# Order of the combinations of h, of the seven products and of the background steps in a hybrid decoder trunk

## The chip, the cores and the metric

The kernel runs on one core of a Trainium2 chip. The metric is the device time of one execution in microseconds (us), the median of several runs. TensorE is called PE in the views, VectorE DVE, ScalarE ACT, GpSimd POOL and SyncE SP; PEld is TensorE's weight load.

## The reference

One layer of a decoder trunk, for 1024 tokens and 16 meta tokens in front of them (1040 rows), model width 1024, all in float32:

```python
h = rmsnorm(concat(meta, x))
glu_a, glu_b, z_conv, q, f, i, g_rec, m_conv, m_rec = split(h @ w_in)      # nine parts of 1024 columns
y_conv = (silu(LN(causal_dwconv31(glu_a * sigmoid(glu_b)))) * silu(z_conv)) @ w_conv_out
y_rec  = (GroupRMSNorm(HGRN2(q, f, i)) * silu(g_rec)) @ w_rec_out          # 8 heads of 128
out    = rmsnorm(x + (sigmoid(m_conv) * y_conv + sigmoid(m_rec) * y_rec) @ w_out)
```

HGRN2 is a gated linear recurrence: per head a forget gate F = lb + (1 - lb) * sigmoid(f), K = 1 - F, q = silu(q_raw), and a state that is worked out in chunks of 64 rows.

## The kernel before, in words

**Products in float32.** Each operand is split into a high part, rounded to fp32r, and the rest. A product is three fp32r matmuls: high by high, low by high, high by low (L320, L323, L324 in `project`; L876, L879, L880 in the units). h is held transposed as eight pairs `hh[k]`, `hl[k]` of 128 x 1056; the columns are the rows of the sequence, in two halves of 528 (LH) up to 1056 (LX).

**Weights.** `load_w` loads a tile of 512 KB into `wraw` (SP, L149, two buffers); ACT makes `whi` (L139) and `-whi` in `wlo` (L140), and a DMA of POOL adds `wraw` to `wlo` in flight (L141). A wraw buffer is free again when that DMA has landed. `whi` and `wlo` have three buffers each.

**Plain jobs.** A list of jobs is worked off in order: for each of eight heads `f_job` (forget gate: sigmoid on ACT, L575, two operations on DVE, L576 and L578) and `q_job` (QD, ACT L596, DVE L597), between them `v_job`s, and at last two tiles of the glu part, `gb_job` and `ga_job` (product with the sigmoid, DVE L640). Each runs `project` over two or four blocks of columns with banks of PSUM from a ring of four. The loads of the next job are issued before a job is executed. After each triple of matmuls `tick` adds its length (3 n / 2400 us for n columns) to counters, and steps three queues of background work: `bg`, the heads of HGRN2 (one step each HG_GAP), whose small matmuls (L342 and others) stand in TensorE's order between the triples and wait for DVE's QD, QX, QY (L377 to L421); `cbg`, the taps of the convolution (DVE, L648, 1024 columns each, 31 to a tile); and `sbg`, `weight_sums` (one DMA each SUM_GAP). A head ends with a normalisation on DVE (L527, tile `on`), transposes on TensorE (L537), a copy on ACT (L538) and a store on POOL (L539, `oT_d`). All steps left of the heads are taken by `drained`, ahead of the last `ga_job`.

**Seven products for eight.** The gate parts (g_rec, m_rec; z_conv, m_conv) and the last six tiles of the glu part are worked out in units, two tiles by two halves of the rows at once, by a Strassen-like scheme with seven products (`strassen`). It needs combinations of the weights and of h. `weight_sums` makes those of the weights in DRAM: loads by SP (L718) and accumulating DMAs by POOL (L720), into `sum_rec`, `sum_glu`, `sum_z`. `h_sums(k)` for k = 0 to 3 makes those of h: it loads two tiles `ha`, `hb` (SP, L733, L734), combines them on DVE (L738 to L741), splits four results on ACT and DVE (L135, L136, tile `tsum`) and stores them to `t_d` 4 to 7 (POOL, L745). `h_load` loads t6, t5 and t4 back (POOL, L753); `h_last` puts t7 over the second half of `hh[k]`, `hl[k]`, k = 0 to 3 (POOL, L760, L761), which no job after the plain ones reads otherwise.

A unit's pieces of weights come by `take`: load (SP, L829), then split on ACT and DVE (L135, L136), or on ACT and a DMA of POOL (L139, L140, L141), seven pieces ahead. The products follow each other in a list (`product(0)` to `product(6)`); after some of them an output leaves through `put`: in the gate units outputs 0 and 1 take a silu (L965) and 2 and 3 a sigmoid (L975), in the glu units 0 and 1 a sigmoid (L941). Silu and sigmoid stand in different tables of ACT; an ACT_TABLE_LOAD stands ahead of each change.

After the units follow the three output projections and the last norm. The order on each engine is fixed when the kernel is built, from the order in which the program lists its work.

Of the kernel before, what the change touches and what calls it, by code (L numbers as in the profile page):

```python
# [13 lines left out]
ALU = mybir.AluOpType  # L14
# [8 lines left out]
LH = 528  # L23
# [10 lines left out]
HG_GAP = 1.85  # L34
CONV_RATE = 0.64
SUM_GAP = 2.4
# [8 lines left out]
def hybrid_kernel(ctx: ExitStack, tc: tile.TileContext, xT, xtok, wv, wp, wro, wco, wout, prm, fg, msk, out):  # L45
# [586 lines left out]
    def ga_job(j):  # L632
        def run(w):
            a = glu.pop(j)
            for blk in project(w, hh, hl, FB):
                yield
                if blk is None:
                    continue
                o, n, ps = blk
                TT(out=a[:, o:o + n], in0=a[:, o:o + n], in1=ps[:, 0:n], op=ALU.mult)  # L640
            conv_start(j, a)
        return run
# [106 lines left out]
    def h_load():  # L749
        for i in (6, 5, 4):  # L750
            for k in range(4):
                t = slot(f"t{i}_{k}", dt=F32R)
                nc.gpsimd.dma_start(out=t, in_=t_d[i][k])  # L753
                tt[i].append(t.rearrange("p (a n) -> p a n", a=2))
        yield

    def h_last():

        for k in range(4):
            nc.gpsimd.dma_start(out=hh[k][:, LH:LX], in_=t_d[7][k][:, 0:LH])  # L760
            nc.gpsimd.dma_start(out=hl[k][:, LH:LX], in_=t_d[7][k][:, LH:LX])  # L761
# [6 lines left out]
    jobs.append(([], h_sums(0)))  # L768
    jobs.append(([], h_sums(1)))
    for j in range(NC):  # L770
        jobs.append(([wp[4, j]], f_job(j)))
        if j == 0:
            jobs.append(([], h_sums(2)))
            jobs.append(([], h_sums(3)))
        jobs.append(([wp[3, j]], q_job(j)))
# [82 lines left out]
    def strassen(m0, cols, put):  # L858
# [43 lines left out]
        Y = banks()  # L902
        yield from product(3, Y, t7)
        w = tmp()
        for c in C:
            TT(out=w[c], in0=v[c], in1=Y[c], op=ALU.add)
        Z = banks()
        yield from product(4, Z, tcomb(5))
        for c in C:
            TT(out=w[c], in0=w[c], in1=Z[c], op=ALU.add)  # L910
            put(3, c, w[c])
        yield from product(5, Y, tcomb(4), False)
        u = tmp()
        for c in C:
            TT(out=u[c], in0=v[c], in1=Y[c], op=ALU.add)
            put(2, c, u[c])
        yield from product(6, Z, b22, False)
        for c in C:
            TT(out=v[c], in0=v[c], in1=Z[c], op=ALU.add)
            put(1, c, v[c])  # L920
# [60 lines left out]
    def add_pair(kind, j, fn):  # L981
# [3 lines left out]
        pieces.extend([a[0, 0], s[1], a[0, 1], s[2], s[0], a[1, 1], s[3]])  # L985
# [187 lines left out]
    h_last()  # L1173
# [149 lines left out]
```

## Time and profile before

| | us |
|---|---|
| three runs | 1268.52, 1276.27, 1275.67 |
| median | 1275.67 |
| the profiled execution | 1267.29 |
| its span in the trace | 1265.5 |
| TensorE busy in the span | 1171.3 |
| DVE, ACT, POOL busy | 874.9, 564.5, 289.9 |

All times below are of that one profiled execution and count from the start of its span. The plain jobs run to about 507 us, the units from there to about 980, the output projections to the end. "Idle before, releaser" is the time that an engine stood still ahead of an instruction, and what it waited for last. PEclk is the clock granted to TensorE, as a share of full speed.

### The profile page before, as it was taken

The numbers are of one execution on the slowest core, as the hardware profiler recorded it, in microseconds if no ns is written. First come the engines' busy times: TensorE is split into PE (matmuls) and PEld (weight loads), VectorE is DVE, ScalarE is ACT, GpSimd is POOL, SyncE is SP. The second block draws the span as 40 slices with busy tenths as digits, with TensorE's granted clock in tenths as the row PEclk, the third lists the DMA queues.
The fourth block names the chain that finished last, engine by engine and source line by source line (L and its number), as shares of the span: only waits on it lengthen the run. The fifth ranks groups of instructions, "written<-read, shape, count | busy, mean of one in ns | idle before, by whom it ended". The sixth has DMA issues, their size and how long they took to land.

```text
span 1265.5 us, 21745 instructions
## 1 busy us (share of the span) xinstructions
PE 1171.3 (93%) x8376; PEld 1011.6 (80%) x8376; DVE 874.9 (69%) x1501; ACT 564.5 (45%) x1043; POOL 289.9 (23%) x376
## 2 busy tenths in 40 slices
PE   8939999999979998769999999999999999999997
PEld 7937788988968898547888888979898778788886
DVE  7547766366355669786799999498989747645444
ACT  7544442433314431336666756666665325222211
POOL 5242120321222131422222223222233131000000
PEclk9978999999989998779999999999999989999999
DMA  6498594898596993999999989989899986445421
GB/s 222 154 285 318 157 223 137 182 240 213 110 251 151 244 193 67 349 289 245 232 244 240 252 221 243 229 200 226 213 225 314 342 233 238 162 128 170 147 88 50
DMA packets 119223, 266.54 MB, mean 211 GB/s; under 512 B 12112, under 2 KB 12496, under 8 KB 119120
## 3 DMA queue, kind: packets, MB, share of 16 engines
q0 software_dynamic: 49264, 123.16, 43.7%
q1 hardware_dynamic: 60496, 125.07, 29.6%
q10 hardware_dynamic: 9360, 16.94, 3.6%
q8 instruction: 65, 1.06, 0.3%
q14 instruction: 38, 0.31, 0.1%
HBM read 169.04 MB, written 95.81 MB: 209 GB/s over the span
## 4 chain that ended last, share of the span: by engine, by line
PE 60%; DMA 14%; DVE 13%; issue 8%; POOL 2%; ACT 2%; SPq 0%; POOLq 0%; DVEq 0%; ACTq 0%
PE mm L320 6%; PE mm L323 6%; PE mm L324 6%; PE hg L876 4%; PE hg L880 4%; PE hg L879 4%; PE mm L876 4%; PE mm L880 4%; PE mm L879 4%; DMA wlo<-wraw 2%; DMA wl<-wr 2%; PE mm L204 2%; PE mm L206 2%; PE mm L205 2%; DVE QX L386 1%
## 5 line engine op out<-in xcount | busy, mean ns | idle before, releaser
L648 DVE SCALAR_TENSOR_TENSOR c<-glu,pt,c 128x1024 f32<-128x1024 f32 (+9 forms) x240 | 306.3, 1278 | 3.5
L320 PE MATMUL mm<-hh,whi 128*128 128x264 f32 (+2 forms) x512 | 164.5, 322 | 21.6 <-ACT F L575 21.2
L141 POOL DMA_DIRECT2D wl<-wr x129 | 111.3, 903 | 312.1 <-ACT wl L140 236.8
L323 PE MATMUL mm<-hl,whi 128*128 128x264 f32 (+2 forms) x512 | 162.5, 318 | 0.3 <-DVE hl L559 0.3
L324 PE MATMUL mm<-hh,wlo 128*128 128x264 f32 (+2 forms) x512 | 161.5, 316 | 0.0
L139 ACT CAST wh<-wr 128x512 fp32r<-128x512 f32 x129 | 79.1, 619 | 111.3 <-PE hg L879 43.0
L320 PEld LDWEIGHTS mm<-hh,whi 128*128 128x128 f32 x512 | 98.1, 192 | 27.9 <-ACT F L575 21.4
L323 PEld LDWEIGHTS mm<-hl,whi 128*128 128x128 f32 x512 | 98.3, 192 | 5.9 <-DVE hl L559 0.7
L324 PEld LDWEIGHTS mm<-hh,wlo 128*128 128x128 f32 x512 | 98.2, 192 | 5.8
L876 PE MATMUL hg<-hh,wh 128*128 128x512 f32 (+1 forms) x224 | 79.7, 356 | 12.1 <-DMA hh<-t_d 12.1
L880 PE MATMUL hg<-hh,wl 128*128 128x512 f32 (+1 forms) x224 | 79.8, 356 | 4.7 <-DVE wl L136 3.8
L135 ACT CAST wh<-wr 128x512 fp32r<-128x512 f32 x63 | 38.6, 619 | 97.4 <-PE mm L323 36.2
L140 ACT ACTIVATE wl<-wh 128x512 fp32r<-128x512 f32 x129 | 79.3, 627 | 4.4 <-DMA gr<-gmr_d 2.2
L876 PE MATMUL mm<-hh,wh 128*128 128x512 f32 (+1 forms) x224 | 78.2, 349 | 1.8 <-ACT wh L135 0.8
L879 PE MATMUL hg<-hl,wh 128*128 128x512 f32 (+1 forms) x224 | 79.9, 357 | 0.0
L880 PE MATMUL mm<-hh,wl 128*128 128x512 f32 (+1 forms) x224 | 77.9, 349 | 0.4 <-DVE wl L136 0.3
L879 PE MATMUL mm<-hl,wh 128*128 128x512 f32 (+1 forms) x224 | 77.8, 347 | 0.0
L141 POOL DMA_DIRECT2D wlo<-wraw x24 | 23.0, 956 | 205.3 <-ACT wlo L140 104.4
L876 PE MATMUL hg<-t,wh 128*128 128x512 f32 (+1 forms) x168 | 59.4, 354 | 2.3 <-ACT wh L135 2.1
L879 PE MATMUL hg<-t,wh 128*128 128x512 f32 (+1 forms) x168 | 59.1, 352 | 0.0
L880 PE MATMUL mm<-t,wl 128*128 128x512 f32 (+1 forms) x168 | 58.4, 348 | 0.6 <-DMA wl<-wr 0.6
L880 PE MATMUL hg<-t,wl 128*128 128x512 f32 (+1 forms) x168 | 58.9, 350 | 0.0
(346 smaller groups left out, 3126.3 us busy)
## 6 DMA issues: line engine op xcount, KB each, us to landing
wl<-wr POOLq DMA_DIRECT2D x129, 256.0 KB, 5.1
wr<-in_wp_dram SPq DMA_DIRECT2D x66, 256.0 KB, 3.9
wlo<-wraw POOLq DMA_DIRECT2D x24, 512.0 KB, 5.6
wraw<-in_wp_dram SPq DMA_DIRECT2D x20, 512.0 KB, 6.6
t_d<-tsum POOLq DMA_DIRECT2D x16, 528.0 KB, 6.7
sum_rec<-in_wp_dram SPq DMA_DIRECT2D x16, 512.0 KB, 11.4
sum_z<-in_wp_dram SPq DMA_DIRECT2D x16, 512.0 KB, 10.3
wr<-sum_rec SPq DMA_DIRECT2D x32, 256.0 KB, 4.8
```

The source lines that it names most:

```text
L135: act.copy(out=hi, in_=src)
L139: act.copy(out=hi, in_=src)
L140: act.activation(out=lo, in_=hi.bitcast(F32), func=AF.Copy, scale=-1.0)
L141: nc.gpsimd.dma_start(out=lo, in_=src, accum_op=ALU.add)
L204: pe.matmul(ps, lhsT=a, rhs=whi, start=first, stop=False, **kw)
L320: mm = pe.matmul(ps[:, 0:n], lhsT=a, rhs=xh[k][:, o:o + n], start=(k == 0), stop=False)
L323: pe.matmul(ps[:, 0:n], lhsT=a, rhs=xl[k][:, o:o + n], start=False, stop=False)
L324: last[:] = [pe.matmul(ps[:, 0:n], lhsT=b, rhs=xh[k][:, o:o + n], start=False, stop=(k == KT - 1))]
L648: dve.scalar_tensor_tensor(out=dst, in0=a[:, p0 - d:L - d], scalar=cw[:, j, TAPS - 1 - d:TAPS - d], in1=dst, op0=ALU.mult, op1=ALU.add)
L876: mm = pe.matmul(ps[c], lhsT=a, rhs=xh, start=start and k == 0, stop=False, skip_group_check=True)
L879: pe.matmul(ps[c], lhsT=a, rhs=xl, start=False, stop=False, skip_group_check=True)
L880: pe.matmul(ps[c], lhsT=b, rhs=xh, start=False, stop=k == 3, skip_group_check=True)
```

## The change

Six edits:

- `HG_GAP` goes from 1.85 to 2.0 and `SUM_GAP` from 2.4 to 2.05.
- `h_sums(0)` and `h_sums(1)` move from ahead of `f_job(0)` to behind it, `h_sums(2)` and `h_sums(3)` from behind `f_job(0)` to behind `q_job(0)`.
- `ga_job` takes its blocks of columns from the last to the first.
- `h_last` is called from `h_load`, between t5 and t4 in the program, no longer right ahead of the units.
- The products are listed as 0, 1, 2, then t5, t7, b22, t4 (before: t7, t5, t4, b22); the outputs leave in the order 0, 3, 1, 2 (before: 0, 3, 2, 1).
- The pieces of weights are listed in the order of the products.

```diff
-HG_GAP = 1.85
+HG_GAP = 2.0
-SUM_GAP = 2.4
+SUM_GAP = 2.05
...
     def ga_job(j):
...
-            for blk in project(w, hh, hl, FB):
+            for blk in project(w, hh, hl, FB[::-1]):
...
     def h_load():
-        for i in (6, 5, 4):
+
+        for i in (6, 5, 7, 4):
             for k in range(4):
+                if i == 7:
+                    h_last(k)
+                    continue
...
-    def h_last():
-
-        for k in range(4):
-            nc.gpsimd.dma_start(out=hh[k][:, LH:LX], in_=t_d[7][k][:, 0:LH])
-            nc.gpsimd.dma_start(out=hl[k][:, LH:LX], in_=t_d[7][k][:, LH:LX])
+    def h_last(k):
+        nc.gpsimd.dma_start(out=hh[k][:, LH:LX], in_=t_d[7][k][:, 0:LH])
+        nc.gpsimd.dma_start(out=hl[k][:, LH:LX], in_=t_d[7][k][:, LH:LX])
...
-    jobs.append(([], h_sums(0)))
-    jobs.append(([], h_sums(1)))
     for j in range(NC):
         jobs.append(([wp[4, j]], f_job(j)))
         if j == 0:
+            jobs.append(([], h_sums(0)))
+            jobs.append(([], h_sums(1)))
+        jobs.append(([wp[3, j]], q_job(j)))
+        if j == 0:
             jobs.append(([], h_sums(2)))
             jobs.append(([], h_sums(3)))
-        jobs.append(([wp[3, j]], q_job(j)))
...
-        Y = banks()
-        yield from product(3, Y, t7)
+        Z = banks()
+        yield from product(3, Z, tcomb(5))
         w = tmp()
         for c in C:
-            TT(out=w[c], in0=v[c], in1=Y[c], op=ALU.add)
-        Z = banks()
-        yield from product(4, Z, tcomb(5))
+            TT(out=w[c], in0=v[c], in1=Z[c], op=ALU.add)
+        Y = banks()
+        yield from product(4, Y, t7)
         for c in C:
-            TT(out=w[c], in0=w[c], in1=Z[c], op=ALU.add)
+            TT(out=w[c], in0=w[c], in1=Y[c], op=ALU.add)
             put(3, c, w[c])
-        yield from product(5, Y, tcomb(4), False)
+        yield from product(5, Z, b22, False)
         u = tmp()
         for c in C:
-            TT(out=u[c], in0=v[c], in1=Y[c], op=ALU.add)
-            put(2, c, u[c])
-        yield from product(6, Z, b22, False)
+            TT(out=u[c], in0=v[c], in1=Z[c], op=ALU.add)
+            put(1, c, u[c])
+        yield from product(6, Y, tcomb(4), False)
         for c in C:
-            TT(out=v[c], in0=v[c], in1=Z[c], op=ALU.add)
-            put(1, c, v[c])
+            TT(out=v[c], in0=v[c], in1=Y[c], op=ALU.add)
+            put(2, c, v[c])
...
-        pieces.extend([a[0, 0], s[1], a[0, 1], s[2], s[0], a[1, 1], s[3]])
+        pieces.extend([a[0, 0], s[1], a[0, 1], s[0], s[2], s[3], a[1, 1]])
...
-    h_last()
```

**ACT, at the first forget gate.** Before, the splits of `h_sums(0)` and of `h_sums(1)` (L135) and the casts of a weight (L139, L140) stood ahead of the sigmoids of `f_job(0)` (L575):

```order
80 L135 CAST tsum<-t_821 128x528
81 L139 CAST whi<-wraw 128x1024
82 L140 ACTIVATE wlo<-whi 128x1024
83 L135 CAST tsum<-hb 128x528
84 L135 CAST tsum<-ha 128x528
85 L135 CAST tsum<-hb 128x528
86 L135 CAST tsum<-t_853 128x528
87 L575 ACT_TABLE_LOAD
88 L575 ACTIVATE F<-mm 128x264 x2
89 L575 ACTIVATE F<-mm 128x256 x2
```

Now, the sigmoids come first, then the first block of `q_job(0)` (L596) and `h_sums(0)`:

```order
77 L575 ACT_TABLE_LOAD
78 L575 ACTIVATE F<-mm 128x264 x2
79 L575 ACTIVATE F<-mm 128x256
80 L139 CAST whi<-wraw 128x1024
81 L575 ACTIVATE F<-mm 128x256
82 L140 ACTIVATE wlo<-whi 128x1024
83 L596 ACTIVATE QD<-mm 128x256x2
84 L135 CAST tsum<-hb 128x528
85 L135 CAST tsum<-ha 128x528
86 L135 CAST tsum<-hb 128x528
87 L135 CAST tsum<-t_942 128x528
```

Eight splits and one pair of casts moved from ahead of the sigmoids of `f_job(0)` to behind them. The sigmoids of `f_job(1)` stand in rows 105 and 106, behind the splits of all four `h_sums`.

**POOL, at the loads of the combinations.** Before, the first pair of t7 (L760, L761) stood in rows 138 and 140 between accumulations (L720); then came twelve t loads (L753), of which the last two are shown, two accumulations and the other pairs of t7:

```order
152 L753 DMA t_2_5776<-t_d 128x1056
153 L753 DMA t_3_5778<-t_d 128x1056
154 L720 DMA sum_z<-sum_z 128x2x512 x2
155 L760 DMA hh_611<-t_d 128x528
156 L761 DMA hl_612<-t_d 128x528
157 L760 DMA hh_639<-t_d 128x528
```

Now, with `h_last` in lines 762 and 763 and `h_load` in 757 of the changed kernel:

```order
138 L720 DMA sum_z<-sum_z 128x2x512 x5
139 L763 DMA hl_588<-t_d 128x528
140 L762 DMA hh_587<-t_d 128x528
141 L762 DMA hh_611<-t_d 128x528
142 L763 DMA hl_612<-t_d 128x528
143 L762 DMA hh_639<-t_d 128x528
144 L763 DMA hl_640<-t_d 128x528
145 L762 DMA hh_667<-t_d 128x528
146 L763 DMA hl_668<-t_d 128x528
147 L757 DMA t_0_5760<-t_d 128x1056
148 L539 DMA oT_d<-oT 128x1024
149 L757 DMA t_1_5762<-t_d 128x1056
```

All five accumulations and all eight transfers of t7 stand ahead of the t loads, and the store of the last head (L539), before at row 135, stands between the first t load and the second.

**DVE, at the end of the last head.** Before, L527 (`on`) stood ahead of the blocks of the last `ga_job` (L640):

```order
612 L114 SCALAR_TENSOR_TENSOR ro<-rt_o,ry_o 128x8
613 L648 SCALAR_TENSOR_TENSOR c_5485<-glu,pt,c_5485 128x1024
614 L527 TENSOR_TENSOR on<-hg,ro 128x512 x2
615 L648 SCALAR_TENSOR_TENSOR c_5485<-glu,pt,c_5485 128x1024 x3
616 L648 SCALAR_TENSOR_TENSOR c_5485<-glu,pt,c_5485 128x1023
617 L640 TENSOR_TENSOR glu<-glu,mm 128x264
```

Now it stands behind all four of them, and the first splits of the units' weights (L136) follow:

```order
635 L648 SCALAR_TENSOR_TENSOR c_5422<-glu,pt,c_5422 128x1020
636 L114 SCALAR_TENSOR_TENSOR ro<-rt_o,ry_o 128x8
637 L640 TENSOR_TENSOR glu<-glu,mm 128x264
638 L527 TENSOR_TENSOR on<-hg,ro 128x512 x2
639 L648 SCALAR_TENSOR_TENSOR c_5422<-glu,pt,c_5422 128x1019
640 L616 TENSOR_SCALAR c_5758<-glu,pt 128x1024
641 L136 TENSOR_TENSOR wl<-wr,wh 128x512 x5
```

Between the last block of the first `ga_job` and L527 stood 13 taps; now 20 stand there. In the order of ACT there are 47 ACT_TABLE_LOADs before and 67 now.

## Rows read from the trace of the kernel before

**Rows 1.** The page of the whole span: its row of TensorE in the engines' shares (busy us, share of the span, instructions), and of the 40 slices the clock row.

```profile
PE 1171.3 (93%) x8376; PEld 1011.6 (80%) x8376; DVE 874.9 (69%) x1501; ACT 564.5 (45%) x1043; POOL 289.9 (23%) x376
...
PEclk9978999999989998779999999999999989999999
```

**Rows 2.** The table of stretches: from and to in us, length, busy us and instructions of each engine, the granted clock (PEclk), the mean busy share of the DMA engines, GB/s.

```profile
76.50:97.80 21.30, 0.09 (x1) 0.10 (x1) 6.35 (x11) 6.15 (x9) 4.56 (x8) 0.61 0.90 290
97.80:123.30 25.50, 25.50 (x208) 22.68 (x209) 19.36 (x38) 10.04 (x18) 6.11 (x10) 0.93 0.86 306
123.30:474.00 350.70, 325.45 (x3871) 293.96 (x3870) 205.69 (x569) 129.18 (x339) 76.54 (x84) 0.98 0.80 193
...
474.00:562.00 88.00, 63.71 (x333) 53.10 (x332) 74.57 (x85) 21.75 (x42) 25.76 (x35) 0.81 0.84 238
...
562.00:960.00 398.00, 394.43 (x2169) 340.55 (x2169) 338.96 (x398) 260.61 (x417) 100.96 (x121) 1.00 0.92 231
```

**Rows 3.** The table of TensorE's waits from 60 to 130 us: who waited for what, us in total, times, the longest.

```profile
PE mm L320 <- ACT F L575: 21.2, 1, 21.2
```

**Rows 4.** The same from 123 to 474 us.

```profile
PE hg L342 <- DVE QD L377: 7.3, 2, 7.1
PE hg L537 <- DVE on L527: 7.2, 4, 2.1
```

**Rows 5.** The same from 470 to 562 us.

```profile
PE hg L876 <- DMA hh<-t_d: 12.1, 1, 12.1
PE hg L537 <- DVE on L527: 5.8, 1, 5.8
PE hg L880 <- DVE wl L136: 3.8, 1, 3.8
PE hg L876 <- ACT wh L135: 2.1, 1, 2.1
```

**Rows 6.** The table of stretches, for four stretches at the lower clock (columns as in rows 2).

```profile
97.70:101.50 3.80, 3.79 (x9) 3.02 (x10) 3.77 (x11) 0.79 (x3) 0.08 (x1) 0.50 0.98 369
364.60:367.80 3.20, 3.20 (x72) 3.08 (x73) 3.20 (x7) 0.00 (x0) 3.20 (x4) 0.50 1.12 292
...
511.80:524.80 13.00, 10.67 (x23) 7.45 (x24) 7.30 (x9) 3.07 (x5) 3.19 (x6) 0.50 1.12 355
547.80:552.10 4.30, 4.30 (x9) 2.34 (x9) 0.10 (x1) 0.09 (x1) 4.16 (x5) 0.50 1.19 302
```

**Rows 7.** The chain of waits, in order of time, of the stretches from 70 to 125 us and from 480 to 560 us: start, length, what.

```profile
70.18 8.64 DMA wlo<-wraw
...
80.58 11.56 DMA hb<-h_d
...
527.06 16.01 DMA sum_z<-sum_z
```

**Rows 8.** The timeline of ACT from 74 to 100 us: start, length, line, operation, tiles, shapes, and in brackets the idle time before it and what ended it.

```profile
93.72 0.63 ACT L135 CAST tsum<-hb 128x528 fp32r<-128x528 f32 x1 [11.42 <-DVE hb L740]
```

**Rows 9.** The timeline of TensorE at three places: the first matmul of `q_job(1)`, of the first unit and of the third.

```profile
123.30 0.39 PE L320 MATMUL mm<-hh,whi 128*128 128x512 f32 x1
...
507.34 0.39 PE L876 MATMUL hg<-hh,wh 128*128 128x512 f32 x1
...
565.07 0.40 PE L876 MATMUL hg<-hh,wh 128*128 128x512 f32 x1
```

**Rows 10.** The timeline of SP's queue from 70 to 100 us, and of the view of the tile `ha` the time of its DMAs from issue to landing (least, median, most).

```profile
79.31 1.18 SPq L733 DMA_DIRECT2D ha<-h_d  x1
...
93.31 0.38 SPq L733 DMA_DIRECT2D ha<-h_d  x1
...
DMA to landing us min/median/max: 3.9/6.7/9.8
```

**Rows 11.** The timeline of DVE from 74 to 100 us: one of the operations of `h_sums` and one of its splits.

```profile
92.98 0.71 DVE L740 TENSOR_TENSOR hb<-ha,hb 128x528 f32<-128x528 f32 x1
...
95.01 0.70 DVE L136 TENSOR_TENSOR tsum<-ha,tsum 128x528 fp32r<-128x528 f32 x1
```

**Rows 12.** The chain of waits from 325 to 370 us.

```profile
335.58 16.99 DMA wlo<-wraw
352.63 7.96 DMA wraw<-in_wp_dram
```

**Rows 13.** The timeline of POOL from 490 to 560 us; the accumulation at 527.06 of rows 7 stands between the last two.

```profile
495.91 0.61 POOL L539 DMA_DIRECT2D oT_d<-oT  x1 [29.86 <-ACT oT L538]
...
507.80 3.84 POOL L753 DMA_DIRECT2D t<-t_d  x5
...
540.81 0.53 POOL L761 DMA_DIRECT2D hl<-t_d  x1 [0.54 <-DMA t<-t_d]
```

**Rows 14.** The timeline of DVE from 468 to 500 us: an update of the state, the last block of the first `ga_job` and a tap.

```profile
469.82 0.35 DVE L504 SCALAR_TENSOR_TENSOR S<-S,PA,hg 128x128 f32<-128x128 f32 x1
...
473.73 0.42 DVE L640 TENSOR_TENSOR glu<-glu,mm 128x256 f32<-128x256 f32 x1 [3.56 <-PE mm L324]
...
484.37 1.28 DVE L648 SCALAR_TENSOR_TENSOR c<-glu,pt,c 128x1024 f32<-128x1024 f32 x1
```

**Rows 15.** The view of line 975, the sigmoid of the gate units: its table loads (count, least, median and most ns, first and last start), and who waited for it (us, times).

```profile
L975 ACT ACT_TABLE_LOAD  x16: 1283/1283/1283, 552.6 to 975.3; - x16
...
  ACT wh L139: 2.9, 6
```

## The prediction, as it stood before the run

> **What bounds the kernel now.** I read the page's engine shares and 40 slices first [rows 1]. TensorE is busy for 1171.3 of 1265.5 us, and the clock row falls below 9 in seven of 40 slices (3, 4, 12, 16, 17, 18 and 33). So there are at most 94 us of idle time and some slow stretches to win, and the question is where they lie. The table of stretches [rows 2] answers it: from 76.5 to 97.8 us TensorE does next to nothing, from 123.3 to 474 it is idle for 25 of 351 us, from 474 to 562 for 24 of 88 at a mean clock of 0.81, and from 562 to 960 for 3.6 of 398. The waits by stretch [rows 3 to 5] name who ends them. After each long wait a stretch at clock 0.50 follows, the lower of the two levels, 1.2 GHz [rows 6]; work done there takes twice its time, so half of the busy time in it is lost: 3.79/2 = 1.9 us after the wait at 97.7, 1.6 after the one at 364.6, 10.67/2 = 5.3 from 511.8 to 524.8, 2.2 after 547.8.
>
> Each of the three first stretches is touched by one part of the change; the fourth only by the new order of the products.
>
> **Part A, the forget gate ahead of the combinations of h.** The wait of 21.2 us is for the first sigmoid of F [rows 3]. The chain of waits goes back from it through a table load, three splits of h_sums(1), and a load of hb that took 11.56 us, which itself was issued only after a wlo transfer of 8.64 us had freed a wraw slot [rows 7]. The ACT rows say the same: the sigmoids stand behind splits that begin at 93.72 [rows 8]. In the changed order F comes first on ACT, so q_job(0) can start as f_job(0) ends, at about 76.6, 21 us sooner and with no slow clock behind it. That is not the gain, since the same four combinations must still be made. They now stand ahead of the sigmoids of f_job(1) on ACT, and q_job(1) needs those for its banks. Its start is the point to compare: 123.30 before [rows 9].
>
> I follow the loads. SP issued the pair of h_sums(1) from 79.31 on [rows 10]; the pair of h_sums(0) now has that place, behind the same slot, and lands near 92. The pair of h_sums(1) takes the place at 93.31 and lands a median 6.7 us on, at 100; that of h_sums(2) goes as soon as its buffers are free, at about 98, and lands near 105. The pair of h_sums(3) waits on SP behind a wv load for a further wraw slot (some 9 us behind the one of 93, as the wlo of 8.64 shows), is issued near 103 and lands near 110. DVE needs 4 x 0.71 + 4 x 0.70 = 5.6 us for each [rows 11], ACT's splits go beside them, and the sigmoids of f_job(1) follow the last split, near 114. That gives about 115 for q_job(1), against 123.3: 8 us, taken as **7.5**. Transfers speak for no more: the DMA engines were 0.90 and 0.86 busy from 76.5 to 123.3 [rows 2], and not a byte is taken away. Lower end 2 (the pair of h_sums(3) lands as late as it did); upper end 14 (the slots come free without a wait behind each other).
>
> **Part B, longer steps for the heads, shorter for the weight sums.** The step of a head is taken when TensorE's work since the last one passes HG_GAP. A triple of matmuls counts 0.33 us at 264 columns, 0.32 at 256 and 0.64 at 512; so 1.85 was reached after 6 triples (3 at 512) and 2.0 after 7 (4). DVE gets 17 to 33% more time for each step. Between 123 and 474 TensorE was idle for 25 us, nearly all of it waiting for DVE's operations of the heads [rows 2, 4]. 7.1 of it is one wait for QD: there a wlo transfer took 16.99 us and a wraw load behind it 7.96, and ACT had no weight to split [rows 12]; longer steps do nothing for it. Of the other 18, in pieces of up to 2.1 us, I count on a third, 6. Against that the sums come every 7 triples instead of 8 in the phases of 264 columns, 13% denser, where the DMA engines have a mean share of 0.80 [rows 2]; I take 2 off. **4**, from -8 (one more event such as that of 357 to 364: 7.1 and 1.6 of slow clock) to 10. The sums also end earlier, and fewer of them stand in part C.
>
> **Part C, from the last plain glu tile to the first units.** Before, POOL's queue was this: two loads and three accumulations of sums with the first t7 pair among them, then all twelve t loads from 507.80 on, two more accumulations, and only then the other three t7 pairs, the last half at 540.81 [rows 13]. The fourth product of unit 0 waited 12.1 us for them [rows 5]. Now the last tile takes its last columns first, so hh and hl may be overwritten while its other columns are still multiplied; all eight t7 transfers go ahead of t5, and t7 is the fifth product. That wait goes, 12.1 and 2.2 of slow clock; so do the 3.8 and 2.1 around 512 and 517 and the 5.3 of slow clock there, if what replaces them is early: 25.5 in all.
>
> What is late next is two things. First, the last head: its transposes (L537) stand behind L527 on DVE, and between ga_job(0)'s end (its last L640, at 473.73 [rows 14]) and L527 DVE now has 20 taps where it had 13. Its queue is 20 x 1.28 = 25.6, seven L504 of 0.35, and about 6 of smaller operations (four L640, the pieces of the square root, L527 itself): L527 is done near 35 us after that point, the transposes near 37, and the first weight of the units, split on DVE behind L527, a tap and L616, near 38. Before, the first product began at 507.34 [rows 9], 33.6 us after. So it is 4 later. Second, t6_1 is issued behind the oT_d store, which waits for that same head (29.86 us of POOL's time before, [rows 13]); it lands 8 to 10 us after, and the first product fills only 12 x 0.23 us of that: a new wait of about 6, and 1.5 for its slow clock. 25.5 - 4 - 7.5 = **14**: the third unit begins 78 us after that point, where it was 91. Lower end 4, if the t loads take as long as the slowest transfers of this stretch (an accumulation took 16.01 us, [rows 7]; the DMA share is 1.12 from 511.8 to 524.8, [rows 6]); upper end 22, if DVE runs ahead and no wait comes.
>
> The Trainium skill (DMA: Bandwidth & Descriptors, Issuing engines are not separate DMA queues) speaks for the lower end: it says that transfers of all issuers end up on the same 16 engines and interleave, so moving a load forward in POOL's queue would slow what SP loads beside it. The share of 1.12 and the 16.01 us agree with it; by that rule alone the sum would be 14 instead of 24.
>
> **Part D, the products' order.** TensorE's work in a unit is the same. ACT's isn't: the outputs now leave in the order silu, sigmoid, silu, sigmoid (put 0, 3, 1, 2), and each of the 16 gate units changes its table four times, where two or three changes did. ACT's order has 67 table loads for 47. A load takes 1283 ns [rows 15], so 20 x 1.283 = 25.7 us more for ACT. From 562 to 960 ACT is busy for 260.6 of 398 us and TensorE waits 3.6 us in all [rows 2]; at 286 of 398 it still has room, and its splits run several pieces ahead. So I cost it at **-1.5**, hidden beside TensorE's work; without that cover it is up to -25.7 (a rival below). Range -6 to 1, the 1 for a bank released one product earlier.
>
> **Sum.** 7.5 + 4 + 14 - 1.5 = 24 us. The profiled execution took 1267.3 us; from it the sum gives 1243. But two of the three timed runs are at 1276, and the median is 1275.67: from it, 1251.7. I predict **1250**.
>
> **Rivals.**
> 1. The waits only move (A by order, C by DVE). For it: the DMA engines are 0.86 to 1.12 busy in both places [rows 2, 6], and L527 gets more taps ahead of it. Against: the loads that TensorE waits for stand many places further forward. A 2, B 2, C 7, D -1: 10 us, 1266.
> 2. All that waits goes. For it: 21.2 + 1.9 in A and 25.5 in C are idle or slow time with TensorE's inputs ready. Against: the part of A that comes back at f_job(1). A 14, B 6, C 19, D -1: 38 us, **1238**.
> 3. Slower: the denser sums take the engines from the weight loads. One mechanism: a wlo accumulation of 17 us holds a wraw slot, ACT has nothing to split, TensorE stands for 7.1 and loses 1.6 of clock, as at 357 [rows 4, 6, 12]. It decides from three further events on (24/8.7 = 2.8); six, one for every second batch of sums, would cost 52 and end 28 slower, at **1304**. For it: 13% more transfers in the same time at a mean share of 0.80 [rows 2]. Against: one such event in 350 us.
> 4. ACT becomes the bound of the units. The 20 further loads stand in front of splits (wh<-wr waits for them in ACT's queue), and if each delays a weight that TensorE needs next, 25.7 come back: no change, **1276**. For it: casts of wh already stood behind the sigmoids of L975 six times, 2.9 us [rows 15]. Against: TensorE waited only 3.6 us in 398 with some 40 loads already there [rows 2].
>
> The Trainium skill (ScalarE: Activation LUTs, Table sets: the hidden batching unit) speaks for rival 4: activations are to be batched by the set of tables they use, and the change does the opposite. In What ACT_TABLE_LOAD costs it gives 1283 ns for the load, as the trace has, and about 1380 ns of drain besides, which no row here shows apart; with it the 20 switches would cost an estimated 53 us of ACT, and 28 slower than before if all of it were on TensorE's path.
>
> **How the numbers follow.** My forecast 0.56, rival 1 0.15, rival 2 0.15, rival 3 0.07, rival 4 0.07. The range leaves out rivals 3 and 4 and a little at the edges: 1230 (38 off the fastest run, 1268.5) to 1270 (6 off the median, rival 1 with a bad B). A measurement of this kernel tells about 1% from no change, 12.7 us: faster than 1263 holds for nearly all of the forecast, rival 2 and some of rival 1, 0.55 + 0.15 + 0.06 = 0.76. Within 1%: the rest of rival 1, most of rival 4 and half-sized events of rival 3, 0.17. Slower 0.07.
>
> **What would show it.** Right: no wait for F at 76 to 98; q_job(1) starting near 115; a clock row without the dip in slice 3; the wait of the products for hh<-t_d gone, one of 5 to 8 us for a t6 load in its place; the third unit's first product, at 565.07 before [rows 9] or 91 us after ga_job(0)'s last L640, now 78 after it; from there to the last unit the same 398 us within 3. Wrong: a wait of over 10 us for F of f_job(1) or for a bank of q_job(1); TensorE waiting for DVE's L527 more than 12 us; several waits for QD of 5 us or more with a wlo transfer before them; waits for wh or wl from ACT through the units that sum to over 8 us.

## The result and the profile after

The changed kernel takes 1231.3 us (four runs, 1229.8 to 1232.9) against 1272.6 (four runs, 1268.5 to 1276.3): 0.968 of the time, 95% interval 0.964 to 0.972. That is 41 us, where I had said 24; the time lies inside the range of 1230 to 1270, 1.3 us above its lower end, and nearer to rival 2 (1238) than to my 1250. Of the profiled executions the span goes from 1265.5 to 1228.2, by 37.3 us, and I divide that.

The page after, the same two rows as [rows 1]: TensorE's busy time and the clock in 40 slices.

```profile
PE 1163.5 (95%) x8376; PEld 1008.0 (82%) x8376; DVE 877.1 (71%) x1501; ACT 588.0 (48%) x1063; POOL 287.6 (23%) x376
...
PEclk9996999999999999899999999999999999999999
```

The dips at slices 12, 16, 18 and 33 are gone and that at 17 is 0.8. Of the first dip slice 3 is back at 0.9, but slice 4 shows 0.6, lower than before (0.8). The table of stretches of the kernel after answers to [rows 2] and [rows 6] (length, busy us of each engine, granted clock, DMA share, GB/s):

```profile
91.00:97.60 6.60, 0.06 (x5) 0.04 (x7) 3.11 (x5) 0.00 (x0) 0.87 (x1) 0.68 0.98 337
97.60:109.40 11.80, 11.80 (x132) 11.50 (x132) 11.73 (x22) 4.63 (x9) 2.69 (x6) 0.75 1.04 373
109.40:121.00 11.60, 0.04 (x2) 0.02 (x1) 5.65 (x10) 4.63 (x8) 4.23 (x7) 0.69 1.01 367
121.00:124.50 3.50, 2.78 (x40) 1.87 (x44) 3.50 (x11) 0.76 (x3) 1.30 (x3) 0.50 0.95 369
121.00:450.70 329.70, 317.95 (x3818) 287.67 (x3819) 205.99 (x564) 123.75 (x326) 81.32 (x91) 0.99 0.87 209
450.70:540.50 89.80, 76.64 (x433) 64.63 (x432) 80.02 (x100) 35.60 (x71) 23.22 (x35) 0.94 0.87 249
540.50:941.10 400.60, 397.61 (x2185) 343.68 (x2184) 350.80 (x408) 277.88 (x427) 105.67 (x131) 1.00 0.93 237
```

TensorE's idle time between q_job(1) and the last block of the first ga_job falls from 25.3 of 350.7 us [rows 2] to 11.8 of 329.7, and its busy time by 7.5 (325.45 and 317.95). Some 6 of that are small matmuls of the last head that now fall behind this point (3818 instructions for 3871): by the timelines, 22 small matmuls of 3.7 us stood between it and the first unit before, 78 of 9.7 us stand there now. The rest, some 1.5 us, is slow clock that is gone (a mean of 0.98 before, 0.99 after). Five places in the timelines divide the 37.3 us; the differences are worked out here:

| start of | before | after | moved by | won in the step | forecast |
|---|---|---|---|---|---|
| q_job(1) | 123.30 | 120.98 | -2.3 | 2.3 | 7.5 |
| last L640 of ga_job(0) | 473.73 | 450.18 | -23.6 | 21.2 | 4 |
| the third unit | 565.07 | 534.92 | -30.2 | 6.6 | 14 |
| last matmul of the units | 975.0 | 941.1 | -34.0 | 3.8 | -1.5 |
| end of the span | 1265.5 | 1228.2 | -37.3 | 3.3 | 0 |

The third unit isn't the same amount of work away in the two kernels: its first matmul is the 133rd of the units before and the 145th after, since the first units are mixed differently in TensorE's order. Counted by matmuls, the 169th starts 100.8 us after ga_job(0)'s last L640 before the change and 90.4 after it, and from there to the last one both kernels take the same time. Before:

```profile
574.50:975.10 400.60, 397.87 (x2185) 343.65 (x2185) 341.83 (x402) 255.67 (x408) 105.57 (x130) 1.00 0.93 235
```

That is the length of 540.50:941.10 after. So at equal work the third step wins 10.4 us and the fourth nothing.

The waits of TensorE after, in the stretch of [rows 3] (60 to 130 us; us in total, times, the longest):

```profile
PE mm L320 <- ACT F L575: 11.6, 1, 11.6
PE hg L342 <- DVE QD L377: 6.5, 1, 6.5
```

The one wait of 21.2 us has become two. In the stretch that answers to [rows 4], 121.5 to 451 us, behind the 11.6 us for F:

```profile
...
PE hg L342 <- DVE QX L395: 3.8, 3, 2.0
PE hg L537 <- DVE on L527: 2.8, 2, 1.5
PE hg L342 <- DVE QY L421: 2.7, 2, 2.0
...
PE hg L342 <- DVE QD L377: 0.2, 1, 0.2
```

The wait of 7.1 us for QD behind a late weight is gone, and the waits for `on` are 2.8 us where they were 7.2. In the stretch that answers to [rows 5], 440 to 545 us (L879 and L883 were L876 and L880):

```profile
PE mm L883 <- DMA wl<-wr: 3.1, 1, 3.1
PE hg L879 <- DVE e L909: 3.0, 1, 3.0
...
PE hg L879 <- DMA t<-t_d: 1.7, 1, 1.7
PE hg L537 <- DVE on L527: 1.5, 1, 1.5
```

No wait for hh<-t_d is left; the t load that I had put at 6 us costs 1.7. POOL's timeline answers to [rows 13] (L720 the sums, L762 and L763 t7, L757 the t loads):

```profile
462.63 1.14 POOL L720 DMA_DIRECT2D sum_z<-sum_z  x1 [3.97 <-DMA sum_z<-sum_z]
472.93 0.60 POOL L763 DMA_DIRECT2D hl<-t_d  x1 [9.16 <-PE mm L324]
...
477.21 0.62 POOL L757 DMA_DIRECT2D t<-t_d  x1
485.39 0.54 POOL L539 DMA_DIRECT2D oT_d<-oT  x1 [7.56 <-ACT oT L538]
485.92 4.40 POOL L757 DMA_DIRECT2D t<-t_d  x8
```

The last accumulation is issued 12.5 us after ga_job(0)'s last L640, where it was 55.3 (529.02 in the trace before). So no accumulation stands among the t loads. The chain of waits ahead of 121 us names the load that q_job(1) waited for:

```profile
107.88 8.96 DMA hb<-h_d
```

It is hb of h_sums(3).

### The profile page after: what moved, and what is told of

Its sections match the earlier page's. It is cut to its first block, busy times and chain, and to the rows that moved or that the text cites. A ratio compares the mean times of both kernels' runs of the same rounds, so it can differ in the third digit from the quotient of the medians.

```text
span 1228.2 us, 21742 instructions
## 1 busy us (share of the span) xinstructions
PE 1163.5 (95%) x8376; PEld 1008.0 (82%) x8376; DVE 877.1 (71%) x1501; ACT 588.0 (48%) x1063; POOL 287.6 (23%) x376
## 4 chain that ended last, share of the span: by engine, by line
PE 73%; DVE 11%; DMA 10%; issue 3%; ACT 1%; POOL 1%; SPq 0%; DVEq 0%; POOLq 0%; ACTq 0%
PE mm L320 8%; PE mm L323 8%; PE mm L324 8%; PE hg L879 5%; PE hg L882 5%; PE hg L883 5%; PE mm L883 5%; PE mm L879 5%; PE mm L882 4%; DVE c L648 2%; PE mm L204 2%; PE mm L206 2%; PE mm L205 2%; DMA hb<-h_d 2%; DMA wr<-sum_rec 1%
## 5 line engine op out<-in xcount | busy, mean ns | idle before, releaser
L648 DVE SCALAR_TENSOR_TENSOR c<-glu,pt,c 128x1024 f32<-128x1024 f32 (+10 forms) x240 | 306.3, 1279 | 3.6
L141 POOL DMA_DIRECT2D wl<-wr x129 | 110.9, 897 | 329.2 <-ACT wl L140 255.2
L320 PE MATMUL mm<-hh,whi 128*128 128x264 f32 (+2 forms) x512 | 166.2, 326 | 12.0 <-ACT F L575 11.6
L139 ACT CAST wh<-wr 128x512 fp32r<-128x512 f32 x129 | 78.1, 618 | 108.4 <-PE hg L882 44.5
L320 PEld LDWEIGHTS mm<-hh,whi 128*128 128x128 f32 x512 | 98.4, 193 | 19.0 <-ACT F L575 11.8
L883 PE MATMUL mm<-hh,wl 128*128 128x512 f32 (+1 forms) x224 | 78.1, 349 | 4.7 <-DMA wl<-wr 4.7
L879 PE MATMUL hg<-hh,wh 128*128 128x512 f32 (+1 forms) x224 | 78.8, 352 | 3.6 <-DVE e L909 3.0
L879 PE MATMUL mm<-hh,wh 128*128 128x512 f32 (+1 forms) x224 | 78.4, 350 | 2.3 <-ACT wh L139 1.9
L140 ACT ACTIVATE wl<-wh 128x512 fp32r<-128x512 f32 x129 | 79.6, 629 | 1.7
L883 PE MATMUL hg<-hh,wl 128*128 128x512 f32 (+1 forms) x224 | 78.4, 350 | 0.4 <-DVE wl L136 0.4
L135 ACT CAST wh<-wr 128x512 fp32r<-128x512 f32 x63 | 38.7, 619 | 51.5 <-PE mm L323 29.2
L879 PE MATMUL hg<-t,wh 128*128 128x512 f32 (+1 forms) x168 | 58.9, 351 | 1.7 <-DMA t<-t_d 1.7
L883 PE MATMUL mm<-t,wl 128*128 128x512 f32 (+1 forms) x168 | 58.9, 351 | 1.0 <-DMA wl<-wr 1.0
L879 PE MATMUL mm<-t,wh 128*128 128x512 f32 (+1 forms) x168 | 59.0, 351 | 0.8 <-ACT wh L135 0.8
L882 PE MATMUL mm<-t,wh 128*128 128x512 f32 (+1 forms) x168 | 58.9, 350 | 0.0
## 6 DMA issues: line engine op xcount, KB each, us to landing
sum_rec<-in_wp_dram SPq DMA_DIRECT2D x16, 512.0 KB, 10.5
```

Source lines behind the costliest of these rows:

```text
L135: act.copy(out=hi, in_=src)
L139: act.copy(out=hi, in_=src)
L140: act.activation(out=lo, in_=hi.bitcast(F32), func=AF.Copy, scale=-1.0)
L141: nc.gpsimd.dma_start(out=lo, in_=src, accum_op=ALU.add)
L320: mm = pe.matmul(ps[:, 0:n], lhsT=a, rhs=xh[k][:, o:o + n], start=(k == 0), stop=False)
L648: dve.scalar_tensor_tensor(out=dst, in0=a[:, p0 - d:L - d], scalar=cw[:, j, TAPS - 1 - d:TAPS - d], in1=dst, op0=ALU.mult, op1=ALU.add)
```

## The experiments

Times are medians; the kernel before had 1271.7, 1273.1, 1274.0 and 1271.6 in the four groups of runs, and intervals are of the ratio to it. The changed kernel was timed in the result's runs only, so a difference from it also carries the 2.4 us by which the kernel before moves from group to group.

**One part alone.** The edits are lines of the change itself:

```diff
# HG_GAP alone                      # SUM_GAP alone
-HG_GAP = 1.85                      -SUM_GAP = 2.4
+HG_GAP = 2.0                       +SUM_GAP = 2.05
# the h_sums alone: behind f_job(0) and q_job(0), as in the change
# the rest alone: ga_job, h_load, h_last, the products and the pieces, as in the change
```

> The kernel before with HG_GAP 2.0 alone. In the trace after the change, 23 of the 37 us were won between q_job(1) and the last gb_job, where I had forecast 4. Theory H (the longer head step gives DVE time, so TensorE's waits for QX, QY, QD and on, and the slow clock behind them, go): 15 to 20 us faster, 1253 to 1258, with idle time of TensorE from 123 to 474 falling from 25 us to about 10. Rival S (the denser weight sums did it, by ending earlier and by falling elsewhere among the weight loads): within 4 us of before. Rival P (the parts that move the phases against each other did it; neither gap alone does): within 6 us, and the wait of 7 us behind a late weight stands at another place.

Measured: 1243.6, ratio 0.979 (0.976 to 0.983), 28 us faster (the profiled executions: 1243.9 for 1265.5). Theory H, and more than it asked. In its trace the stretch from q_job(1) to ga_job(0)'s end is 329.3 us, as after the whole change (329.2), where it was 350.4. Of TensorE's waits from 123 to 455 us:

```profile
PE hg L342 <- DVE QX L395: 3.0, 2, 1.9
...
PE hg L342 <- DVE QY L421: 2.1, 2, 1.9
...
PE hg L342 <- DVE QD L377: 0.2, 1, 0.2
```

The 7.1 us for QD are gone here too.

> The kernel before with SUM_GAP 2.05 alone. Theory H: within 4 us of before, or up to 8 slower by one more wait for a late weight. Rival S: 10 to 18 us faster, with fewer accumulations of sums standing among the t loads near 510 us. My prediction on record took 2 us off for it.

Measured: 1251.5, ratio 0.985 (0.982 to 0.989), 20 us faster. Theory H allowed 4: it falls as an account of the whole, and S is right that the sums matter, but not where S had them: that stretch is 347.7 us, 2.7 shorter. What shrinks are the first units. No accumulation stands among its t loads, and of TensorE's waits in [rows 5] the first is halved (470 to 562 us):

```profile
PE hg L537 <- DVE on L527: 5.9, 1, 5.9
PE hg L876 <- DMA hh<-t_d: 5.7, 1, 5.7
PE hg L880 <- DVE wl L136: 3.9, 1, 3.9
```

> The kernel before with the four h_sums moved alone (behind f_job(0) and q_job(0)). The trace after the change shows TensorE waiting 6.5 us for QD and 11.6 us for F of f_job(1) where it had waited 21.2, and the job behind q_job(1) only 1 us sooner. Theory W (the wait only moves, to the sigmoids of f_job(1) behind the splits of h_sums(3)): 0 to 3 us faster. Forecast on record: 7.5 faster. Rival P (the shift keeps the weight loads of the later jobs out of the sums' way): 8 us or more faster, won behind 140 us.

Measured: 1257.0, ratio 0.990 (0.986 to 0.994), 15 us faster, against W. q_job(1) starts at 120.6, only 2.7 sooner, as W says; the rest is won behind it, the wait for QD near 357 down to 2.7 us and the last head in time ahead of the units. That is rival P.

> The kernel before with the other half alone: the last glu tile from its last columns on, t7 loaded ahead of t5 and t4, and the new order of the products (h_sums and both gaps as before). By the trace after the change, 10 us are won between the last gb_job and the third unit, none in the units, 3 behind them. Theory (part C is its own, as forecast, smaller by 4): 8 to 14 us faster. Rival (C needs the sums to be finished by then, which the gaps bring): 0 to 4 us faster, with accumulations still standing ahead of the t loads. On the tables: 20 more table loads cost nothing, the units from the third on take 400 us as before, within 2.

Measured: 1262.3, ratio 0.993 (0.990 to 0.996), 9 us faster. The profiled execution, at 1269.9, is the longest but one of its ten, so I take its order and not its sizes; where the 9 us are won it doesn't show. On the tables: from the 169th matmul of the units to the last it takes 396.7 us, no longer than before. The time is the first theory's, the trace the rival's: seven of the eight t7 loads do stand ahead of the t loads, but sums still stand between them and behind (POOL's timeline of this kernel), and the first units gain nothing:

```profile
507.66 2.28 POOL L720 DMA_DIRECT2D sum_z<-sum_z  x1
...
515.90 1.82 POOL L757 DMA_DIRECT2D t<-t_d  x3 [1.46 <-DMA sum_z<-sum_z]
...
534.96 2.46 POOL L720 DMA_DIRECT2D sum_z<-sum_z  x2 [1.19 <-DMA t<-t_d]
...
550.28 1.17 POOL L720 DMA_DIRECT2D sum_z<-sum_z  x1 [11.41 <-DVE c L648]
```

The parts win 28 + 20 + 15 + 9 = 72 us alone and 41 together. So each wins something that another wins too, and a part has to be priced from the other end as well.

**One part taken back.**

```diff
# of the changed kernel, one at a time
-HG_GAP = 2.0          +HG_GAP = 1.85
-SUM_GAP = 2.05        +SUM_GAP = 2.4
# ga_job, h_load, h_last, products and pieces as before
# the h_sums as before
```

> The changed kernel with HG_GAP back at 1.85. Alone, HG_GAP 2.0 gave 28 us (22 by the profile, 18 of it between q_job(1) and the last glu tiles), SUM_GAP 20, the moved h_sums 15, the rest 9: 72 in all where the whole change gives 41, so they share something. Theory H (the head step is what wins the stretch of the plain jobs; the others win there only the one wait of 7 us for QD behind a late weight, which any shift removes): 12 to 18 us slower than the changed kernel, 1243 to 1249, with the waits for on, QX and QY of 1.5 to 2 us back. Rival (all wins are that one collision and the like): at most 6 slower.

Measured: 1245.7, ratio 0.978 (0.976 to 0.981), 14 us slower than the changed kernel. Theory H. TensorE's waits from 121 to 472 us of this kernel:

```profile
PE hg L342 <- DVE QY L421: 5.8, 5, 1.9
PE hg L342 <- DVE QX L395: 5.6, 5, 1.7
PE hg L342 <- DVE QD L377: 5.2, 2, 4.2
```

They are 16.6 us in twelve pieces, where the changed kernel has 6.7 in six. The stretch from q_job(1) to ga_job(0)'s end is 352.6 us, no shorter than before the change: HG_GAP wins all of it. Some 10 of these 23 us it gives back behind that point: from there to the 169th matmul of the units this kernel takes 80.8 us and the changed one, with more of the last head still to do, 90.4.

> The changed kernel with SUM_GAP back at 2.4. Theory S (the stretch around the first units is decided by how many accumulations of sums still stand in POOL's queue among the t loads, since in the kernel with SUM_GAP 2.05 alone the products' wait for hh<-t_d fell from 12.1 to 5.7 us, and with the t7 loads ahead but the sums as before nothing was won there): 6 to 12 us slower than the changed kernel, 1237 to 1243, lost between 451 and 545 us. Forecast on record (the order of the loads is what wins there): within 3 of the changed kernel, or 2 faster.

Measured: 1241.8, ratio 0.975 (0.972 to 0.977), 10 us slower. Theory S in the main: of the 10.5 us between the profiled executions 7.9 are lost from ga_job(0)'s end to the 169th matmul of the units, where S had them all, and 4.7 ahead of it (what lies behind is 1.3 shorter). With all t7 loads and t5 ahead as changed, the waits are back (445 to 560 us):

```profile
PE hg L879 <- DMA t<-t_d: 9.6, 1, 9.6
PE hg L879 <- DVE e L909: 8.3, 1, 8.3
```

> The changed kernel without its third part: the last glu tile, the loads of t and the products as before, both gaps and the moved h_sums as changed. Theory S: 0 to 5 us slower than the changed kernel, 1231 to 1236, since the sums are out of POOL's queue by then anyway. Forecast on record: 14 slower, 1245, with the wait for hh<-t_d of about 12 us back.

Measured: 1243.2, ratio 0.975 (0.971 to 0.979; runs 1236 to 1245), 12 us slower. Neither account holds: the wait for hh<-t_d that the forecast wanted back is not there, and S had at most 5. From the first unit's start to the 169th matmul of the units it takes 59.0 us, 3 more than the changed kernel; the loss is behind that, 1.7 in the units and 6.7 in what follows them.

> The changed kernel with the four h_sums where they were, ahead of and behind f_job(0). Theory W (the first wait only moved): within 3 us of the changed kernel, 1228 to 1234, the wait of 21 us for F back ahead of q_job(0), and the two of 6.5 and 11.6 us gone. Forecast on record: 7.5 slower, 1239. Rival P (its shift keeps the weight loads apart): 6 or more slower, lost behind 145 us.

Measured: 1230.9, ratio 0.967 (0.964 to 0.970): the same as the changed kernel. Theory W: TensorE's one wait for F is 20.7 us, and q_job(1) starts at 121.7, where the changed kernel has 121.0. The move of the h_sums is worth 15 us by itself and nothing in the company of the others. The wait for QD near 357 is 0.2 us in both traces; that the others had removed what the move removes alone is a reading of that, and accounts for part of the 15.

**What decides the first units.** In the ten kernels so far I counted the accumulations of weight sums that have not landed when the last ga_job ends (its last L640), and took the time from the first unit's start to its 169th matmul (both from the timelines; the rest alone by its long execution):

| | sums not landed | first unit to 169th matmul, us |
|---|---|---|
| before; HG_GAP alone; h_sums alone; the rest alone; SUM_GAP taken back | 5; 4; 5; 6; 5 | 67.2; 65.1; 70.2; 70.5; 63.9 |
| the rest taken back | 0 | 59.0 |
| changed; SUM_GAP alone; HG_GAP, h_sums taken back | 0 | 56.0; 54.9; 54.9; 55.8 |

The four kernels that follow have none either, and 52.1 to 55.9 us. SUM_GAP, which gets the sums out of the way, is worth 8 us here in the changed kernel (63.9 to 56.0) and 12 in the one before (67.2 to 54.9). The order of the t loads is worth 3 at most (59.0 to 56.0): SUM_GAP alone has the old order, and 54.9.

**The outputs' order.**

```diff
-        yield from product(5, Z, b22, False)
+        yield from product(5, Y, tcomb(4), False)
...
-            put(1, c, u[c])
+            put(2, c, u[c])
# and b22, put(1) last; the pieces accordingly
```

> The changed kernel with t4 ahead of b22 again, so that the outputs leave in the order 0, 3, 2, 1 as before; t5 still stands ahead of t7. ACT has about 20 table loads less. Theory (table loads of ACT lie beside TensorE's work): within 3 us of the changed kernel, 1228 to 1234, the units from the third to the last within 1 us of 400.6. Rival 4 of the prediction (they cost TensorE time): 5 to 25 faster. A third case: the order b22 before t4 itself gains by t4's late load or by the last unit's outputs: 3 to 8 slower.

Measured: 1239.0, ratio 0.973 (0.970 to 0.975), 8 us slower: the third case. With fewer table loads the units take longer, not shorter: from the 169th matmul to the last there are 41 for 58. That stretch in this kernel (the changed one has 540.50:941.10 above):

```profile
540.10:944.90 404.80, 399.78 (x2184) 344.95 (x2183) 350.09 (x409) 257.23 (x411) 105.18 (x130) 1.00 0.92 233
```

ACT has 20.7 us less to do, 257.2 for 277.9, and TensorE needs 404.8 us for 400.6; behind the units 3.4 more are lost. This order isn't the one of the kernel before (t5 still stands ahead of t7), which needs 400.6 us there as the changed one does. What in it holds TensorE up was not settled by a run of its own: its trace shows waits for ACT's copies (L897, 2.3 us) and for a DVE operation (L909, 1.2) in the units, where the changed kernel has 0.4 for both.

**Further along the way that the runs point.**

```diff
-HG_GAP = 2.0
+HG_GAP = 2.4
```

> The changed kernel with HG_GAP 2.4: 8 triples to a step instead of 7 at 264 and 256 columns, 4 as before at 512. 1.85 to 2.0 won 14 us here. Theory H (steps are too dense for DVE; each us of wait left, 11 from 145 to 451, is a step taken too early): the waits for QX, QY and on fall further, 3 to 8 faster, if the last head still ends in time. Rival (the last head then ends behind the last ga_job and the units wait for it): 5 to 20 slower, with the wait at L537 of over 5 us ahead of the first unit.

Measured: 1224.6, ratio 0.962 (0.959 to 0.964), 7 us faster than the changed kernel. Both effects are there: the stretch to ga_job(0)'s end is shorter by 4, and the wait for the last head ahead of the units grows from 1.5 to 7.2 us.

```diff
-        if j == 0:
-            jobs.append(([], h_sums(0)))
-            jobs.append(([], h_sums(1)))
         jobs.append(([wp[3, j]], q_job(j)))
-        if j == 0:
-            jobs.append(([], h_sums(2)))
-            jobs.append(([], h_sums(3)))
+        if 1 <= j <= 4:
+            jobs.append(([], h_sums(j - 1)))
```

> The changed kernel with the h_sums further back: h_sums(0) to h_sums(3) stand one each behind q_job(1) to q_job(4), where before and after the change all four stand within the first three jobs. Putting them behind f_job(0) moved the wait of 21 us for F to two of 6.5 (QD) and 11.6 us (F of f_job(1)) and won nothing. Theory Q (what keeps TensorE waiting there are their eight loads in SP's queue behind wraw slots, and their work ahead of the next sigmoids and QD): both waits go, 18 us and some 3 of slow clock, against up to 6 for DVE's 22 us of work among the heads: 10 to 18 us faster than the changed kernel, 1213 to 1221. Rival (the transfers of the first 120 us or the weights are what limits there, whoever asks): within 5 us, with waits for wh, QD or QX in their place.

Measured: 1246.1, ratio 0.978 (0.975 to 0.980), 15 us slower than the changed kernel. Neither: q_job(1) starts at 106.3, 14.7 us sooner, the two waits gone, and it all comes back later. TensorE's waits from 150 to 460 us, and of the view of the tile `hb` who stood idle for it (us, times) and the time from issue to landing:

```profile
PE hg L537 <- DVE on L527: 9.6, 1, 9.6
PE hg L516 <- ACT S L502: 9.4, 1, 9.4
PE hg L342 <- DVE QD L377: 7.8, 1, 7.8
```

```profile
  DVE hb L740: 30.8, 4
...
DMA to landing us min/median/max: 8.6/14.9/18.4
```

Three waits of 8 to 10 us, each behind a pair of h that DVE or ACT stands waiting for in the middle of a head's work. The chain of waits has the pair of the first one:

```profile
158.34 18.35 DMA hb<-h_d
```

So the loads were taken out of the h_sums and issued two jobs earlier, with HG_GAP at 2.4:

```diff
+    def h_pre(k):
+        def run(w):
+            held[k] = slot("ha"), slot("hb")
+            nc.sync.dma_start(out=held[k][0], in_=h_d[k])
+            nc.sync.dma_start(out=held[k][1], in_=h_d[k + 4])
+            yield
+        return run
...
         jobs.append(([wp[4, j]], f_job(j)))
+        if j < 4:
+            jobs.append(([], h_pre(j)))
         jobs.append(([wp[3, j]], q_job(j)))
+        if 1 <= j <= 4:
+            jobs.append(([], h_sums(j - 1)))
```

> The changed kernel with HG_GAP 2.4 and the h_sums one each behind q_job(1) to q_job(4), but with the loads of ha and hb for each issued two jobs earlier, behind f_job(0) to f_job(3). With the late h_sums alone the first three jobs became 20 us shorter, and 35 came back later in waits of 8 to 10 us behind DVE operations that stood waiting for hb (18.4 us from issue to landing). Theory Q2 (a DVE operation that waits for a late load holds the head's operations behind it; the load ahead of time frees them): the 20 us stay won, with 1205 to 1214 (HG_GAP 2.4 alone: 1224.6). Rival (the transfers of these stretches are too many for the DMA engines wherever they are issued): 1222 to 1240, with waits for QD, S or on of over 5 us back.

Measured: **1203.7** (1202.5 to 1207.1), ratio 0.946 (0.942 to 0.951): 68 us faster than before, 28 than the changed kernel, the fastest of the study. Q2, and 1 us more than it asked. Its waits from 60 to 480 us and its page's clock row:

```profile
PE hg L537 <- DVE on L527: 5.5, 1, 5.5
PE hg L342 <- DVE QY L421: 2.6, 2, 2.4
PE hg L885 <- DMA t<-t_d: 2.6, 2, 2.4
```

```profile
PEclk9999999999999998899999999999999999999999
```

The waits for F and QD of [rows 3] and of the kernel after are gone, and with them the dip in slices 3 and 4. The loads of hb took a median of 8.2 us, as in the changed kernel, and the longest 16.1, where the changed kernel had 9.0; only nobody stood behind them. Two things are not apart here. HG_GAP differs from the kernel with late h_sums (2.4 for 2.0, worth 7 us by itself), and the loads now run from 79 to 205 us, so that the first jobs have fewer transfers beside them, at a DMA share of 0.65 where the changed kernel has 0.98 to 1.04 from 91 to 121 us:

```profile
76.00:121.00 45.00, 43.01 (x463) 36.67 (x462) 25.33 (x61) 17.19 (x28) 3.08 (x5) 1.00 0.65 202
```

## Why the prediction was right, and where its sum was not

The direction and the range were right. Of the three parts that were to win, B and C did and A did not; the sizes were wrong throughout, and the misses partly cancel: A gave 5 us less than said at q_job(1), C some 4 less, B 17 more. That the time still fell into the range is in part luck, and rival 2, whose time was nearer, has the parts no better (A 14, B 6, C 19).

**Part A was over-sized: 7.5 said, 2.3 measured at q_job(1) and 0 in the time** (the h_sums taken back: no difference; alone they won 15, most of it behind q_job(1)). The wait did move to the sigmoids of f_job(1), as written there, and at 11.6 us it passed the 10 that I had named as a sign of being wrong. The step that failed is the landing of the last pair: I had it issued near 103 and landed near 110. It was issued at 107.9, since the wv load ahead of it went at 105.1, and took 9.0 us to 116.8, at a DMA share of 1.01. Then the slow clock that I had written off as gone came back behind each of the two waits: 11.8 us at 0.75 and 3.5 at 0.50. The lower end was 2, and rival 1's account of A holds. The last two runs show what stood there: the loads' place in the program. The bytes are the same with q_job(1) starting at 104 or 106; they come later, and so fewer at a time.

**Part B is the term that was most mis-sized: 4 said, 21 measured, 15 without the matmuls that fall later.** I counted on a third of the waits in that stretch. More than half of the idle time went (25.3 to 11.8 us) and with it some 1.5 us of slow clock, and HG_GAP alone does it. I had priced each wait by itself; as I read it, DVE's lag carries over from step to step (no run takes a single step apart). The wait of 7.1 us, of which I wrote that longer steps do nothing for it, went too: to 0.2 with HG_GAP alone, to 1.7 with SUM_GAP alone and to 2.7 with the h_sums alone, and it stayed, at 6.9, with the rest alone. That three unrelated edits each take most of it away speaks for a coincidence of transfers, and I had taken it as fixed. The denser sums, on which I took 2 off and built rival 3, cost no wait that the traces show.

**Part C: 14 said, 6.6 measured to the third unit (84.7 us after that point; my own sum gives 77, written as 78), 10.4 at equal work.** The mechanism was half right. The first product begins 34.4 us after ga_job(0)'s last L640; I had 38, from 20 taps, and DVE's queue came out nearly as worked (L527 done 33 us after, where I had 35). The new wait for t6 was 1.7 us, not 6. One reading of POOL's queue was wrong: what I called two loads of sums are accumulations too, so five stood ahead of the t loads. And I had priced the stalls of the old order at 25.5 as if they all went; 13.2 us of idle time and a clock of 0.94 are still there, behind wl, wh and DVE. The credit, too, belongs elsewhere: less to the place of t7 in the queue than to SUM_GAP, which gets the sums out of it in time (8 to 12 us, against 3 at most for the order). I had that in one sentence at the end of part B, without a price.

The rule of the Trainium skill (DMA: Bandwidth & Descriptors, Issuing engines are not separate DMA queues) spoke for the lower end of C, and here the runs agree: t loads moved forward won little there as long as the sums ran beside them (a wait of 9.6 us for a t load with SUM_GAP taken back, 63.9 us to the 169th matmul); fewer transfers at that time did.

**Part D: -1.5 said, 0 measured in the units; against the order with t4 ahead of b22 the new one wins about 8.** The cover that I named holds: 18 more table loads from the 169th matmul to the last than in the kernel before come with 22.2 us more of ACT, and TensorE's time there stays at 400.6. The Trainium skill's rule (ScalarE: Activation LUTs, Table sets: the hidden batching unit) to batch by table set spoke for rival 4; the measurement decides against it for this kernel, where ACT has 30% of the units' time to spare and fewer loads, in the one other order that was run, came out slower. What I missed, as I read it, is that the order of products also sets when each bank and each output comes free; I gave that 1 us at most. No run takes that apart.

**The end.** 3.3 us behind the units were in no part of the sum. Kernels with the new outputs' order take 286 to 289 us there, those with the old one 289 to 294; most of the old ones have one or two waits of 1 to 2 us for ACT's L135 there that the new ones lack or have under 1 us. Why that goes with the outputs' order stays open.

## What to carry to other kernels

When several edits each relieve waits of one in-order pipeline, price them alone and by taking them back: here 72 us alone, 36 by taking back, 41 together. An instruction that waits for a load held all that its engine had behind it, here on DVE and ACT, so a load belongs a few jobs ahead of its first reader; the late readers then cost nothing that the waits show. Background steps that come a little too early for their engine cost more here than I read from the single waits; try their spacing before counting waits.

## What was not expected of the hardware

- A few transfers of 512 KB weigh on all beside them: with four to six of the weight sums not landed when the last ga_job ends, the first 168 matmuls of the units took 64 to 71 us, with none 52 to 59.
- ACT_TABLE_LOADs, 58 for 40 from the 169th matmul to the last, show no slowing of TensorE (400.6 us both before and after the change), at 69% busy of ACT.
- The same transfer's time from issue to landing depended on where it stood: hb of the h_sums took 5.3 to 9.0 us in the changed kernel, 8.6 to 18.4 in the one with late h_sums, among the sums.
